# Memory heads: sample rows turned by VectorE and DMA, the sample memory update moved behind the outputs, and the last key block's high and low queries in one matmul

## The chip, the core and the metric

The kernel runs on one core of a Trainium2 chip. TensorE (PE) multiplies, VectorE (DVE), ScalarE (ACT) and GpSimd (POOL) compute elementwise, and SyncE (SP) issues nearly all DMAs from one in-order queue. The metric is the device time of one execution in microseconds (us); lower is better. All data are 32-bit floats. A product that needs more precision than one pass of the matmul gives is made of three: each factor is split into a high part (the rounded value, names ending in `h`) and a low part (the rest, names ending in `l`), and high x high, high x low and low x high are accumulated.

## The reference

One step of a one-layer streaming encoder over 512 prompt rows and 32 sample rows (they come ahead of the prompt rows, so each tile has 544 columns, T). The change lies in the mLSTM branch, four heads of 512 channels each:

```python
s = jnp.einsum('bhtd,bhsd->bhts', q, k) * dmat
num = w_inter[..., None] * jnp.einsum('bhed,bhtd->bhte', C, q) + jnp.einsum('bhts,bhse->bhte', s, v)
den = w_inter * jnp.einsum('bhd,bhtd->bht', n, q) + jnp.sum(s, axis=-1)
h = num / jnp.maximum(jnp.abs(den), jnp.exp(-m_t))[..., None]
C_new = decay[..., None, None] * C + jnp.einsum('bhs,bhse,bhsd->bhed', w_last, v, k)
```

Here `dmat` holds the decays and is zero for keys later than the query, `C` and `n` are the memory, and `w_inter`, `w_last` and `decay` weigh old memory against new. The prompt starts from an empty memory; the sample has a given one (`C0`). Each head's output `h` is then normalised over its 512 channels, scaled, gated by `z` and multiplied by `w_brm`. The new memories of the prompt (`Cp`) and of the sample (`Cs`) are outputs too.

## The kernel before

Channels lie on the 128 partitions and rows along the free axis; a head has KH = 4 channel tiles `f` and NB = 4 blocks `b` of 128 prompt rows. The heads run one after the other. A head makes its decays (`stage_decay`), keys and queries (`stage_k`, `stage_q`), scores (`stage_scores`), and then its memory chain `mchain(h, pump)`, followed by `stage_br`, the product with `w_brm`.

PE's order is written out by hand. `mchain` is a generator: each `yield n` lets the pump emit n steps of the input projection, about six matmuls of 272 columns each (tile `d`, line 575, 455 for the first head's last), before the chain's next piece. So the tables of gaps (KTGAP, KWGAP, VTGAP, GAPS) set how much projection work stands between two pieces of the chain. The order on the other engines is made by a scheduler from the program's order and priorities. The projection's weights arrive as raw pieces (`wi..r`, line 172, on SP), are summed and split on DVE (lines 508 and 205) and ACT (line 204) and then multiply.

The pieces of a head, in PE's order, with the tiles that the traces name:

- `sc` (line 1054): the scores, one group for each of the four key blocks. Block j has as many query columns as remain behind it: 512, 384, 256 and, for the last, 128. Each group is 12 matmuls: 4 channel tiles times the 3 pairs of high and low. DVE multiplies by the decays (`dm`, line 1062).
- `vt` (line 1210): the prompt's values, turned from channels-on-partitions to rows-on-partitions by PE, four 128x128 transposes for each of 4 blocks; ACT evicts the high part `vh` (line 1213), DVE the low part `vl` (line 1214). They go through two double banks (`paux`), so that a block's transposes wait for the evictions of the block two ahead.
- `vts` (line 1222): the same for the 32 sample rows. POOL first writes them three times side by side (`thrice`, line 963, into `vsm`), so that four transposes give 96 rows, from which `vs` (line 1226 and following) is made, a factor of `Cs` and of the sample's output.
- `nm` (lines 1313, 1289, 1287): the outputs of the prompt's four row blocks and of the sample. `Cs` (line 1241): the sample's memory update, 8 single matmuls a head into a bank of the ring `pd` (shared with `d`); DVE adds each to the old memory (line 1243) and SP stores it (line 1245). In the function `new_memory` they are put between the `nm` matmuls.
- DVE and ACT make the normalisation from the sums (lines 1264 to 1347).
- `C` (line 1112): the prompt's memory. Heads 1 and 2 run it between output and normalised output, with keys fetched by `fetch` (line 1155) and weighed by `parted` (line 1146); head 0 before the outputs, and head 3 in another place.
- `yt` (lines 1366, 1367): the normalised outputs turned back to channels-on-partitions, for each channel tile four transposes of the prompt's blocks and one of the sample's; DVE scales and adds them to `c` (lines 1372, 1373) and multiplies by the gate (line 1374).

## Time and profile before

| | |
|---|---|
| median of 3 runs | 1096.51 us (1095.8 to 1096.66) |
| profiled execution | 1097.29 us, span 1095.6 us |
| granted TensorE clock | 0.999 of full speed |
| PE busy | 1086.1 us, 8765 instructions |
| DVE busy | 920.7 us |
| ACT busy | 684.8 us |
| POOL busy | 180.9 us |
| four heads with their chains | about 90 to 590 us of the span |

A row of a timeline gives the start in us, the duration, the engine, the line and operation, the written and read tiles with their shape, how many instructions were merged, and in brackets the idle time just before, with what ended it. Matmuls are pipelined: a 272-column matmul lasts 0.28 us in the trace while the next begins 0.12 us after it. So what a matmul costs PE is read from the distance of two starts, not from its duration, and the bracket shows a stall's length less that overlap.

### The profile page before, as it was taken

Reading aid. Unit: us, or ns where it says so; the run is one execution under the profiler, and the core shown is the slowest. Engines: PE = TensorE matmul, PEld = TensorE weight load, DVE = VectorE, ACT = ScalarE, POOL = GpSimd, SP = SyncE. Lnnn points to the kernel's source line nnn. Section 1 sums busy time; section 2 is a strip of 40 time slices with the busy share of each in tenths; the row PEclk is TensorE's granted clock in tenths of the full one; section 3 lists DMA queues with packets and bytes.
Section 4 is the critical chain, followed back from the end, with each engine's and each line's share of the span. In section 5 each row is a group of like instructions: output and inputs, shape, how many; then the busy total and the mean of one; then the engine's idle time right before and its main releaser. Section 6 shows DMA issues by size and latency. Waiting matters only on the chain.

```text
span 1095.6 us, 23704 instructions
## 1 busy us (share of the span) xinstructions
PE 1086.1 (99%) x8765; PEld 1075.6 (98%) x8765; DVE 920.7 (84%) x1991; ACT 684.8 (63%) x1545; POOL 180.9 (17%) x417
## 2 busy tenths in 40 slices
PE   9999999999999999999999999999999999999998
PEld 9999999999999999999999999999999999999998
DVE  6986999669798697886899699999999888789885
ACT  6686656645666465665565367777777767445762
POOL 2212014211020120201300123322332100000000
PEclk9999999999999999999999999999999999999999
DMA  6233225533366344374356322222222343443743
GB/s 225 78 97 100 91 87 166 140 106 118 122 182 181 85 145 145 101 244 112 129 186 210 110 78 77 64 84 77 85 77 74 121 158 117 122 129 116 256 146 121
DMA packets 104780, 138.67 MB, mean 127 GB/s; under 512 B 35764, under 2 KB 43572, under 8 KB 104664
## 3 DMA queue, kind: packets, MB, share of 16 engines
q1 hardware_dynamic: 104496, 137.10, 40.2%
q8 instruction: 69, 1.13, 0.4%
q14 instruction: 47, 0.39, 0.1%
q10 hardware_dynamic: 168, 0.06, 0.0%
HBM read 110.96 MB, written 26.16 MB: 125 GB/s over the span
## 4 chain that ended last, share of the span: by engine, by line
PE 76%; DVE 3%; issue 1%; DMA 0%; ACT 0%; POOL 0%; ACTq 0%; DVEq 0%; POOLq 0%
PE d L575 39%; PE ya L229 6%; PE pg L2100 4%; PE yb L229 4%; PE C L1112 3%; PE q L229 3%; PE pl L1816 2%; PE k L229 2%; PE sc L1054 2%; PE nm L1313 2%; PE ple L229 1%; DVE ws L508 1%; PE su L1913 1%; PE ho L1936 1%; PE ht L1896 1%
## 5 line engine op out<-in xcount | busy, mean ns | idle before, releaser
L592 ACT COPY t<-d 128x272 f32<-128x272 f32 x126 | 47.5, 377 | 22.2 <-PE d L575 22.1
L1771 ACT COPY kmos<-hkq 128x256 f32<-128x256 f32 x56 | 24.0, 429 | 50.6 <-DVE hkq L1837 42.9
L1837 DVE TENSOR_TENSOR hkq<-hkq,hq 128x288 f32<-128x288 f32 (+1 forms) x96 | 41.5, 438 | 1.7
L801 DVE SCALAR_TENSOR_TENSOR cv<-ub,vec,cv 128x547 f32<-128x547 f32 x48 | 37.1, 782 | 0.4
L1816 PE MATMUL pl<-hkq,kmos 128*128 128x128 f32 x224 | 34.8, 276 | 0.0
L1816 PEld LDWEIGHTS pl<-hkq,kmos 128*128 128x128 f32 x224 | 30.1, 189 | 0.4 <-ACT kmos L1771 0.4
L1112 PE MATMUL C<-vh,kwl 128*128 128x256 f32 x96 | 27.0, 281 | 0.0
L1112 PE MATMUL C<-vl,kwh 128*128 128x256 f32 x96 | 26.9, 280 | 0.0
L1112 PE MATMUL C<-vh,kwh 128*128 128x256 f32 x96 | 26.8, 279 | 0.0
L963 POOL COPY vsm<-vt 128x96 f32<-128x96 f32 x16 | 16.4, 1035 | 58.6 <-DVE vt L599 43.9
L1853 DVE COPY_PREDICATED at<-lmask,pl 128x256 f32<-128x256 uint8 x56 | 24.9, 444 | 0.0
L1392 DVE TENSOR_TENSOR y<-ya,y 128x272 f32<-128x272 f32 x48 | 18.8, 435 | 7.0 <-PE ya L229 6.7
L1313 PE MATMUL nm<-vh,sh 128*128 128x256 f32 x80 | 22.6, 283 | 0.4 <-ACT Co L1124 0.4
L793 POOL COPY uo<-ub 128x3 f32<-128x3 f32 x16 | 17.8, 1112 | 30.6 <-DVE ub L601 23.5
L1313 PE MATMUL nm<-vl,sh 128*128 128x256 f32 x80 | 22.5, 282 | 0.0
L1313 PE MATMUL nm<-vh,sl 128*128 128x256 f32 x80 | 22.5, 281 | 0.0
L1324 ACT COPY y<-nm 128x516 f32<-128x516 f32 x16 | 9.4, 589 | 20.9 <-PE nm L1313 20.9
L1068 ACT CAST sh<-dm 128x512 fp32r<-128x512 f32 (+3 forms) x16 | 7.3, 459 | 22.8 <-DVE dm L1062 22.8
L1054 PE MATMUL sc<-q,kh 128*128 128x512 f32 (+3 forms) x80 | 18.6, 321 | 0.0
L1243 DVE SCALAR_TENSOR_TENSOR c<-c,wi,Cs 128x256 f32<-128x256 f32 (+1 forms) x32 | 15.0, 474 | 4.1 <-PE Cs L1241 4.0
L1112 PEld LDWEIGHTS C<-vh,kwh 128*128 128x128 f32 x96 | 18.1, 189 | 0.0
L1112 PEld LDWEIGHTS C<-vl,kwh 128*128 128x128 f32 x96 | 18.1, 188 | 0.0
(5764 smaller groups left out, 5141.4 us busy)
## 6 DMA issues: line engine op xcount, KB each, us to landing
ya_d<-y SPq DMA_DIRECT2D x32, 272.0 KB, 3.0
y<-ya_d SPq DMA_DIRECT2D x24, 272.0 KB, 3.0
c<-in_C SPq DMA_DIRECT2D x16, 258.0 KB, 3.5
out_Cs<-c SPq DMA_DIRECT2D x16, 258.0 KB, 2.6
out_Cp<-Co SPq DMA_DIRECT2D x15, 258.0 KB, 2.7
k_d<-kf SPq DMA_DIRECT2D x48, 68.0 KB, 2.0
x<-in_xT SPq DMA_DIRECT2D x8, 272.5 KB, 4.6
ya<-ya_d SPq DMA_DIRECT2D x8, 272.0 KB, 4.3
```

The source lines that it names most:

```text
L229: PE.matmul(both[b][:m, :TH], part(w, off + k * step, m, x), xx[:, half(b)], start=(k == 0 and j == 0), stop=(k == n - 1 and j == 2),)
L575: PE.matmul(ps, ww[:, c], xx, start=(start and k == 0 and j == 0), stop=end, skip_group_check=not start,)
L592: S.copy(t, ps)
L801: last = V.scalar_tensor_tensor(cv[:, :547], ub[:, j : j + 547], vcol(V_CW + 4 * ft + j), cv[:, :547], ALU.mult, ALU.add)
L1054: PE.matmul(pn[:, 0, :n], ks[f][x][:, j * P : (j + 1) * P], qs[f][y][:, NS + j * P : T], start=(f == 0 and i == 0), stop=(f == KH - 1 and ...
L1112: PE.matmul(pn[g], kw[b][x][:, f * P : (f + 1) * P], vv[b][y][:, VS[g]], start=(b == 0 and j == 0), stop=(b == NB - 1 and j == 2),)
L1313: PE.matmul(pn[:, g, VP[g] : VP[g] + VN[g]], st[j][x][:, (i - j) * P : (i - j + 1) * P], vv[j][y][:, VS[g]], start=(j == 0 and q == 0), st ...
L1771: S.copy(km.rearrange("p (n j c) -> p n j c", j=2, c=c), view(kk, HB, ((2 * c, NA // (2 * c)), (c - HB, 2), (1, c))),)
L1816: PE.matmul(pn[:, b * P : (b + 1) * P].rearrange("p (n j c) -> p j n c", j=2, c=c), km[:, b * P : (b + 1) * P], view(qq, b * P, ((HB + c, ...
L1837: V.tensor_tensor(x, x, t, ALU.mult)
L1853: V.copy_predicated(blocks2(at[:, :NA]), twice(lmask[:, li, :P]), blocks2(pn[:, :NA]))
L2100: PE.matmul(ps, part(w, k * P, P, x), xx[:, c], start=(k == 0 and j == 0), stop=(k == KD - 1 and j == 2))
```

## The change

1. **Sample values.** In heads 1 to 3 the `vts` transposes and POOL's three copies go. DVE turns the sample columns of each value tile in 32x32 blocks (`V.transpose`, 128x32, 4 a head); four DMAs write them to DRAM (`vs_d`) so that they lie row by row, and three DMAs read these 32 rows into three stripes of 32 partitions (`vr`). `vs` is made from `vr`. Head 0 keeps its transposes.
2. **Sample outputs.** In all heads the fifth transpose of each `yt` group goes. DVE turns the normalised sample block in place (32x512, one a head); one DMA writes it to DRAM (`ys_d`) and one reads it back as four channel tiles (`ys`). Line 1373's scaling now reads `ys`.
3. **Order in heads 1 and 2.** The eight `Cs` matmuls leave the `nm` loop. A table ORDER spreads them, the fetch and weighing of the keys, the four `C` blocks and the read of `ys` among the projection steps behind `nm`.
4. **Last key block.** Where a high and a low query tile lie side by side in one tile (all four channel tiles in head 0, two in the others), one matmul of 256 columns takes both against the high key; the low key's remains with 128. The two halves of the bank are then added: ACT copies one (`dl`), DVE adds the other.
5. **Gaps.** One step fewer or more at several places (KTGAP, VTGAP of heads 0 and 1, GAPS, the `yield` ahead of the old memory's split).

```diff
-FIRSTK, KTGAP, KWGAP = (3, 2, 1, 1, 1), (6, 14), (6, 3, 11)
-VTGAP = ((2, 1, 1, 1, 1), (1, 1, 1, 1, 1), (1, 1, 1, 1, 1), (0, 2, 2, 1, 1))
-GAPS = (20, 20, 20, 14)
+FIRSTK, KTGAP = (3, 2, 1, 1, 1), (4, 14)
+VTGAP = ((2, 1, 2, 1, 1), (1, 1, 2, 1, 2), (1, 1, 1, 1, 1), (0, 2, 2, 1, 1))
+GAPS, CGAP = (18, 20, 20, 15), 1
+YREAD = 8
+VSREAD = 2
+ORDER = (
+    ("fetch", 1),
+    ("cs", 1),
+    ("cs", 1),
+    ("cs", 1),
+    ("cs", 3),
+    ("cs", 2),
+    ("cs", 1),
+    ("cs", 2),
+    ("part", 0),
+    ("cs", 3),
+    ("mem", 0),
+    ("mem", 0),
+    ("reads", 5),
+    ("mem", 0),
+    ("mem", 0),
+)
+LASTGAP = 3
...
+        dl = d2[:, 384 + NS : 512 + NS]
...
-                qh, ql = pair_tile(f"q{i}", 1)
+                both = xp.tile([P, 2 * T], F32R, tag="x1", name=f"q{i}")
+                qhl = both.rearrange("p (a t) -> p a t", a=2)
+                qh, ql = both[:, :T], both[:, T:]
...
+            beside = [f for f in range(KH) if j == NB - 1 and qs[f][2] is not None]
+            for f in beside:
+                PE.matmul(
+                    pn[:, 0, : 2 * P].rearrange("p (a t) -> p a t", a=2),
+                    ks[f][0][:, j * P : (j + 1) * P],
+                    qs[f][2][:, :, NS + j * P : T],
+                    start=(f == 0),
+                    stop=(f == beside[-1]),
+                )
             for f in range(KH):
                 for i, (x, y) in enumerate(((0, 0), (0, 1), (1, 0))):
+                    if f in beside and x == 0:
+                        continue
                     PE.matmul(
                         pn[:, 0, :n],
                         ks[f][x][:, j * P : (j + 1) * P],
                         qs[f][y][:, NS + j * P : T],
                         start=(f == 0 and i == 0),
                         stop=(f == KH - 1 and i == 2),
+                        skip_group_check=bool(beside),
                     )
             with tc.high_priority():
-                V.tensor_tensor(dj[j], pn[:, 0, :n], dj[j], ALU.mult)
+                if beside:
+                    S.copy(dl, pn[:, 0, n : 2 * n])
+                    V.tensor_tensor(dl, pn[:, 0, :n], dl, ALU.add)
+                V.tensor_tensor(dj[j], dl if beside else pn[:, 0, :n], dj[j], ALU.mult)
...
+    ys_d = [dr.tile([HD, NS], F32, name=f"ys_d{h}") for h in range(MH)]
+    vs_d = [dr.tile([NS, HD], F32, name=f"vs_d{h}") for h in range(MH)]
...
+        if h:
+            vq = small("vsm", [P, KH, 3, NS], bufs=1)[:, :, 0]
+            for f in range(KH):
+                V.transpose(vq[:, f], vt[f][:, :NS])
+            to = vs_d[h].rearrange("t (f q e) -> t f q e", f=KH, e=NS)
+            for q in range(P // NS):
+                nc.sync.dma_start(to[:, :, q, :], vq[q * NS : (q + 1) * NS])
         for b in range(NB):
             yield VTGAP[h][b]
+            if h and b == VSREAD:
+                vr = slot(f"vr{h}")[: 3 * NS, :HD]
+                for i in range(3):
+                    nc.sync.dma_start(vr[i * NS : (i + 1) * NS], vs_d[h])
...
-        pt = paux(f"vts{h}")
-        vsm, copied = triple(vt, "vsm", t["copied"])
-        for f in range(KH):
-            PE.transpose(pt[: 3 * NS, 0, f * P : (f + 1) * P], vsm[:, f], ident)
+        if h == 0:
+            vr = paux(f"vts{h}")[: 3 * NS, 0, :]
+            vsm, copied = triple(vt, "vsm", t["copied"])
+            for f in range(KH):
+                PE.transpose(vr[:, f * P : (f + 1) * P], vsm[:, f], ident)
         vs = small("vs", [3 * NS, VW], F32R, bufs=1)
         with tc.high_priority():
-            S.copy(vs[:, :HD], pt[: 3 * NS, 0, :])
+            S.copy(vs[:, :HD], vr)
...
-        yield 4
+        yield 5
...
-            G.memset(ysm[:, :HD], 0.0)
...
-                if parts and i and (h or i > 1):
+                if parts and i > (1 if h == 0 else 0) and not turns:
...
+            V.transpose(ysm[:NS, :HD], ysm[:NS, :HD])
+        nc.sync.dma_start(ys_d[h].rearrange("(n e) t -> e n t", e=NS), ysm[:NS, :HD].rearrange("p (n t) -> p n t", t=NS))
...
+        def fetch_all():
             for b in range(NB):
                 fetch(b)
-            yield KWGAP[0]
+        def weigh_all():
             for b in range(NB):
                 parted(b)
-            yield KWGAP[1]
-            for f in range(KH):
-                for _ in memory(h, f, kw, vv):
-                    pass
+        def one_memory():
+            for _ in memory(h, blocks.pop(0), kw, vv):
+                pass
+        def turned_sample():
+            ys = slot(f"ys{h}")[:, : KH * NS]
+            nc.sync.dma_start(ys.rearrange("p (f t) -> p f t", f=KH), ys_d[h].rearrange("(f p) t -> p f t", p=P))
+            return [ys[:, f * NS : (f + 1) * NS] for f in range(KH)]
+        todo = {
+            "fetch": fetch_all,
+            "part": weigh_all,
+            "mem": one_memory,
+            "cs": lambda: new_memory(*parts.pop(0)),
+            "reads": lambda: ysmp.extend(turned_sample()),
+        }
+        ysmp = []
+        if 0 < h < MH - 1:
+            for name, gap in ORDER:
+                if gap:
+                    yield gap
+                todo[name]()
+        else:
+            yield GAPS[h] - YREAD
+            ysmp = turned_sample()
 
         hs = []
         for f in range(KH):
-            yield max((KWGAP[2] if 0 < h < MH - 1 else GAPS[h]) if f == 0 else 1, pump.when["z", f] - pump.done)
+            yield max((LASTGAP if 0 < h < MH - 1 else YREAD) if f == 0 else CGAP, pump.when["z", f] - pump.done)
             ft = h * KH + f
             pt = paux(f"yt{ft}")
             for b in range(NB):
                 PE.transpose(pt[:, 0, b * P : (b + 1) * P], yb[b][:, f * P : (f + 1) * P], ident)
-            PE.transpose(pt[:, 1, :P], yb[NB][:, f * P : (f + 1) * P], ident)
...
-            V.scalar_tensor_tensor(c[:, :NS], pt[:, 1, :NS], g, c[:, :NS], ALU.mult, ALU.add)
+            V.scalar_tensor_tensor(c[:, :NS], ysmp[f], g, c[:, :NS], ALU.mult, ALU.add)
```

How the instructions stand after the change (the digits behind a tile's name are head and tile; those behind the underscore are buffers).

PE, head 1, within the outputs; before:

```order
L1313 MATMUL nm11_3983<-vh10_3809,sl10_3411 128x260
L1241 MATMUL Cs100_3990<-vs_3905,kws_3532 128x256
L1313 MATMUL nm11_3983<-vh11_3827,sh11_3428 128x256
L1313 MATMUL nm11_3983<-vl11_3828,sh11_3428 128x256
L1313 MATMUL nm11_3983<-vh11_3827,sl11_3429 128x256
L1313 MATMUL nm11_3983<-vh11_3827,sh11_3428 128x260
L1313 MATMUL nm11_3983<-vl11_3828,sh11_3428 128x260
L1313 MATMUL nm11_3983<-vh11_3827,sl11_3429 128x260
L1241 MATMUL Cs101_3999<-vs_3905,kws_3532 128x260
L1313 MATMUL nm12_4009<-vh10_3809,sh10_3410 128x256
```

PE, head 1, behind the outputs, where the `Cs` matmuls stand now:

```order
L595 MATMUL d361_3705<-xh3_613,ws436l_3922 128x272
L1295 MATMUL Cs100_4185<-vs_3931,kws_3521 128x256
L595 MATMUL d381_3893<-xh0_525,wa1238h_3944 128x272
L595 MATMUL d381_3893<-xl0_526,wa1238h_3944 128x272
L595 MATMUL d381_3893<-xh0_525,wa1238l_3945 128x272
L595 MATMUL d381_3893<-xh1_529,wa1238h_3944 128x272
L595 MATMUL d381_3893<-xl1_530,wa1238h_3944 128x272
L595 MATMUL d381_3893<-xh1_529,wa1238l_3945 128x272
L1295 MATMUL Cs101_4198<-vs_3931,kws_3521 128x260
L595 MATMUL d381_3893<-xh2_533,wa1238h_3944 128x272
```

Each pair of `Cs` had six `nm` matmuls between it; now the distances are 6, 6, 18, 12, 6, 12 and 18 projection matmuls, and the first stands 12 projection matmuls behind the last `nm`. Head 2 has the same distances.

PE, head 1, the scores of the last key block; before (two rows stand for two matmuls each):

```order
L1054 MATMUL sc13_3448<-q10_3206,kh100_3027 128x128 x2
L1054 MATMUL sc13_3448<-q10_3206,kl100_3028 128x128
L1054 MATMUL sc13_3448<-q11_3238,kh101_3066 128x128 x2
L1054 MATMUL sc13_3448<-q11_3238,kl101_3067 128x128
L1054 MATMUL sc13_3448<-qh12_3282,kh110_3117 128x128
```

and now:

```order
L1078 MATMUL sc13_3453<-q10_3211,kh100_3032 128x256
L1078 MATMUL sc13_3453<-q11_3243,kh101_3071 128x256
L1089 MATMUL sc13_3453<-q10_3211,kl100_3033 128x128
L1089 MATMUL sc13_3453<-q11_3243,kl101_3072 128x128
L1089 MATMUL sc13_3453<-qh12_3287,kh110_3122 128x128
```

Twelve matmuls became ten in heads 1 to 3 and eight in head 0.

SP, head 1, around the way of the sample's outputs; before:

```order
L1128 DMA out_Cp<-Co10_4272 128x516
L172 DMA wi10r1_4452<-in_w_in 128x512
L172 DMA wbm10r0_4758<-in_w_brm 128x512
L1128 DMA out_Cp<-Co11_4300 128x516
L1128 DMA out_Cp<-Co12_4328 128x516
L1128 DMA out_Cp<-Co13_4356 128x516
L172 DMA wbm10r512_4760<-in_w_brm 128x512
```

and now:

```order
L1167 DMA out_Cp<-Co10_4386 128x516
L1167 DMA out_Cp<-Co11_4414 128x516
L1402 DMA ys_d1_140<-y14_4082 32x16x32
L192 DMA wbm11r0_4853<-in_w_brm 128x512
L192 DMA wbm11r512_4855<-in_w_brm 128x512
L1421 DMA ys1_4461<-ys_d1_140 128x4x32
L192 DMA wbm12r0_4941<-in_w_brm 128x512
L1167 DMA out_Cp<-Co12_4488 128x516
L1167 DMA out_Cp<-Co13_4516 128x516
```

The write and the read of the sample's outputs stand behind two stores of the prompt's memory and ahead of the other two, with raw pieces of `w_brm` between them. PE has 38 matmuls fewer in all, DVE 20 instructions more, ACT 4 more, POOL 16 fewer, and SP 29 DMAs more.

12 lines of the change are left out of this document (7 added, 5 removed).

## The prediction

> **What bounds the kernel now.** I read the page first: the busy line and the chain that ended last.
>
> ```profile
> span 1095.6 us, 23704 instructions
> PE 1086.1 (99%) x8765; PEld 1075.6 (98%) x8765; DVE 920.7 (84%) x1991; ACT 684.8 (63%) x1545; POOL 180.9 (17%) x417
> PE 76%; DVE 3%; issue 1%; DMA 0%; ACT 0%; POOL 0%; ACTq 0%; DVEq 0%; POOLq 0%
> ```
>
> PE is busy in 99% of the span and carries most of the chain. So a PE instruction that goes is worth the distance to the next start, and every other edit is worth the PE stall it ends or makes. DVE, with 84%, is the engine that can turn into the bound in one stretch or another. Then I read PE's waits.
>
> ```profile
> PE vt L1210 <- DVE vl L1214: 1.4, 3, 0.7
> PE Cs L1241 <- DVE c L1243: 0.9, 2, 0.7
> ```
>
> Of PE's waits these two, `vt` and `Cs`, stand where the change moves something. The view counts only time in which PE shows nothing at work. A matmul lasts 0.28 us while the next starts 0.12 us behind it, so each stall is longer by starts, and short ones do not appear at all. I therefore size them from the timelines.
>
> **The change part by part.** Everything is summed from starts.
>
> *Scores of the last key block.* PE's timeline in head 3, the end of the third group, the start and the end of the fourth:
>
> ```profile
> 520.35 0.28 PE L1054 MATMUL sc<-qh,kh 128*128 128x256 f32 x1
> ...
> 521.05 0.33 PE L1054 MATMUL sc<-q,kh 128*128 128x128 f32 x2
> ...
> 522.34 0.47 PE L1073 MATMUL scs<-qf,ksm 128*96 128x32 f32 x4
> ```
>
> Six of 256 columns take 521.05 - 520.35 = 0.70 us, 0.117 each. Twelve of 128 columns take 522.34 - 521.05 = 1.29 us, 0.1075 each. The change takes away 20 of the narrow and adds 10 of the wide: 20 x 0.1075 - 10 x 0.117 = 0.98 us less. Half the columns hardly save time here, and that is why joining two pays.
>
> A rule speaks against this. The Trainium skill, "TensorE: Matmul & The Clock Gate", section "Part 2: What happens when you issue a matmul", says that a stream of matmuls costs its columns, one a cycle, 55.6 ns measured for 128. By it a wide matmul costs two narrow ones and this term would be 0, the time 1 us longer than mine. The rows above disagree with it (107.5 against 117 ns), and I take the rows.
>
> *Transposes.* Head 3, the sample's values and two groups of the outputs:
>
> ```profile
> 551.47 0.28 PE L575 MATMUL d<-xh,wa1146l 128*128 128x272 f32 x1
> 551.61 0.61 PE L1222 MATMUL vts<-ident,vsm 128*96 128x128 f32 x4
> 551.97 0.38 PE L575 MATMUL d<-xfh,ws144h 128*128 128x272 f32 x1
> 552.19 0.29 PE L575 MATMUL d<-xfl,ws144h 128*128 128x272 f32 x1
> ...
> 579.76 0.60 PE L1366 MATMUL yt<-ident,y 128*128 128x128 f32 x4
> 580.20 0.27 PE L1367 MATMUL yt<-ident,y 128*128 128x128 f32 x1
> 580.23 0.37 PE L575 MATMUL d<-xh,wa1248h 128*128 128x272 f32 x1
> ```
>
> From 551.47 to 552.19 are 0.72 us, of which two `d` at 0.12 (a row of windows below: 235 instructions in 28.00 us) would take 0.24; a `vts` group costs 0.48, three of them 1.44. Five `yt` take 0.47 and four `vts` 0.36: the fifth is worth 0.11, sixteen of them 1.76. So the PE work that goes is 0.98 + 1.44 + 1.76 = 4.18 us.
>
> *New memory of heads 1 and 2.* First and last `Cs` in the `nm` loop of head 1, then of head 2, each with the first stall and the `d` that follows the loop:
>
> ```profile
> 262.31 0.28 PE L1313 MATMUL nm<-vh,sh 128*128 128x260 f32 x1
> ...
> 262.67 0.28 PE L1241 MATMUL Cs<-vs,kws 96*128 96x256 f32 x1
> ...
> 263.92 0.39 PE L1241 MATMUL Cs<-vs,kws 96*128 96x260 f32 x1 [0.25 <-DVE c L1243]
> ...
> 273.12 0.28 PE L575 MATMUL d<-xfh,wa2236h 128*128 128x272 f32 x1
> ...
> 409.69 0.28 PE L1241 MATMUL Cs<-vs,kws 96*128 96x256 f32 x1
> ...
> 411.34 0.39 PE L1241 MATMUL Cs<-vs,kws 96*128 96x260 f32 x1 [0.65 <-DVE c L1243]
> ...
> 420.38 0.28 PE L575 MATMUL d<-xfh,wa2240h 128*128 128x272 f32 x1
> ```
>
> Between 262.67 and 273.12 lie 74 matmuls, 8 `Cs` and 66 `nm`. At 0.12 (three from 262.31 to 262.67) they need 8.88 us and take 10.45: 1.57 lost. In head 2 the same 74 take 10.69: 1.81 lost. Together 3.38 us. The reason is that each `Cs` waits until DVE has read the one before it, and six `nm` give it only 0.72 us while DVE is also at work on the sums of `y`. The change puts 6 to 18 projection matmuls between them. What it costs there, by a `Cs` with its eviction in the timeline and two stretches of the view by windows (length, then busy us and count of PE, its weight loads, DVE, ACT and POOL):
>
> ```profile
> 270.24 0.28 PE L1241 MATMUL Cs<-vs,kws 96*128 96x260 f32 x1
> 270.56 0.48 DVE L1243 SCALAR_TENSOR_TENSOR c<-c,wi,Cs 128x260 f32<-128x260 f32 x1 [1.12 <-PE Cs L1241]
> 246.00:262.00 16.00, 15.71 (x130) 15.50 (x129) 15.75 (x28) 11.16 (x23) 4.78 (x9) 1.00 0.29 98
> 274.00:302.00 28.00, 28.00 (x235) 28.00 (x234) 20.02 (x58) 19.06 (x35) 2.09 (x9) 1.00 0.38 123
> ```
>
> DVE, waiting for nothing else, starts 0.32 us behind a `Cs` and takes 0.48: a round of about 0.86 with the hand-over. A `Cs` and six `d` give 7 x 0.12 = 0.84 us, three times a head, a tie; 12 and 18 give 1.6 us and more. DVE is busy 20.02 of 28 us behind the outputs, so it will often be free. Its keys' weighing (`kwl`, 0.75 us each, four) stands among the evictions and may hold one. From below 0 (all on time), from above 0.9 a head (one whole round lost); I take 0.25 a head, 0.5 in all, nearer the lower end because of the free DVE. Net 2.9 us gained.
>
> *Values.* Two stalls that the added steps cover, and one that nothing covers:
>
> ```profile
> 256.04 0.28 PE L575 MATMUL d<-xfh,ws336l 128*128 128x272 f32 x1
> 256.61 0.66 PE L1210 MATMUL vt<-ident,vt 128*128 128x128 f32 x4 [0.28 <-DVE vl L1214]
> 257.02 0.37 PE L575 MATMUL d<-xh,wa1138h 128*128 128x272 f32 x1
> 257.23 0.28 PE L575 MATMUL d<-xl,wa1138h 128*128 128x272 f32 x1
> ...
> 115.61 0.66 PE L1210 MATMUL vt<-ident,vt 128*128 128x128 f32 x4 [0.40 <-DVE vl L1214]
> ...
> 402.42 0.66 PE L1210 MATMUL vt<-ident,vt 128*128 128x128 f32 x4 [0.74 <-DVE vl L1214]
> ```
>
> From 256.04 to 257.23 are 1.19 us where an undisturbed group of four takes 0.72: 0.47 lost. Its bracket shows 0.28, so the starts lose about 0.18 more than a bracket; head 0 lost 0.40 + 0.18 = 0.58, head 2 0.92. Heads 0 and 1 get another step, about 0.75 us of projection, ahead of the third block. I book 1.05 us for the two. Head 2's gaps are as before; I book nothing, and keep 0.92 as a possible gain.
>
> *DVE's added work.* Prices of the nearest forms:
>
> ```profile
> L1373 DVE SCALAR_TENSOR_TENSOR c<-yt,vec,c 128x32 f32<-128x32 f32 x16 | 3.8, 246 | 0.0
> L975 DVE STREAM_TRANSPOSE kf<-kf 128x544 f32<-128x544 f32 x12 | 8.9, 738 | 0.5
> ```
>
> A 128x32 transpose is taken as 0.25 us, four a head 1.0; the one of 32x512 as 0.7; the add of 128x128, between the two in size, as 0.3. Around the values DVE is full (15.75 of 16 us), so up to 1.0 us a head, 3 in all, could reach PE through the weights; nothing if DVE has caught up until then, as its 20.02 of 28 us behind them lets it. I take 0.4. ACT's four copies and POOL's lighter load lie beside PE's work, for 0.
>
> *The DMA trips.* Written pieces are 128 bytes long. The nearest are the keys' trip with pieces as short (KB each, us to landing), the wait that SP can add (in total, times, longest), and the time between the last scaling of head 1's outputs and the first use of the sample's:
>
> ```profile
> k_d<-kf SPq DMA_DIRECT2D x48, 68.0 KB, 2.0
> kr<-k_d SPq DMA_DIRECT2D x9, 64.0 KB, 4.2
> SPq L172 <- DVE ws L533: 58.3, 20, 5.8
> 285.17 1.44 DVE L1347 TENSOR_SCALAR y<-y,stat,rs 128x512 f32<-128x512 f32 x3
> 301.32 0.24 DVE L1373 SCALAR_TENSOR_TENSOR c<-yt,vec,c 128x32 f32<-128x32 f32 x1
> ```
>
> The sample's output is normalised at about 286.6 and needed at 301.3, 14.7 us later. The trip is 0.7 (turning) + 2.0 + 4.2 = 6.9 us and leaves 7.8 for SP. The values' rows have the same 6.2 us of trip, and from the first `vt` block to the first use of `vs` PE has more than 100 instructions at 0.12, 12 us. I book 0, and from above a late read is the rival below.
>
> *Sum.* -4.18 - 3.38 + 0.5 - 1.05 + 0.4 = -7.7 us. The profiled execution took 1097.29, so it would be 1089.6; it lay 0.8 above the median of 1096.51, which gives 1088.8. With the best ends (-0.5, -0.4, -0.92) 1087.0; with the `Cs` rounds at 1.8, DVE's work at 2.0 and half of the `vt` gain 1092.2.
>
> **The rivals.** *The stalls move.* Only the PE work goes. The `Cs` rounds, now between weight preparation and `kwl` on DVE, lose as much as before, and `vt` waits likewise: 1096.5 - 4.2 = 1092.3. For it: three of the seven distances are a tie. Against it: DVE's free third there.
>
> *DVE bounds the values' stretch.* With 15.75 of 16 us busy, the heads' d stream would go as fast as DVE makes weights. Then what PE saves just ahead of and in this stretch (scores 0.98, `vts` 1.44, `vt` 1.05) is waited away and 1.0 us a head comes on top: -1.76 - 3.38 + 0.5 + 3.0 = -1.6, or 1094.9. For it: the full window. Against it: PE lost only 0.29 us of 16 in that window.
>
> *Slower: the sample's output comes late.* The four scalings that read `ys` stand on DVE ahead of those of the prompt. If the read, queued on SP behind two memory stores and raw pieces, is late, DVE stands, with it the gates and splits that `stage_br` multiplies, and weights. One SP wait of the raw pieces' longest kind (5.8) at the write and one at the read make 11.6, 3.8 more than the 7.8 us free. In four heads this is 15.2 - 7.7 = 7.5 us slower, 1104. It decides from 1.9 us a head, 9.7 us of SP waits. Against it: both waits would have to be long in each head.
>
> The Trainium skill, "DMA: Bandwidth & Descriptors", section "Specifications", says that transfers below 512 bytes are read, modified and written; were the trip longer by that, this rival would gain. The keys' writes of that size landed in 2.0 us, so the trace shows no such loss.
>
> **How the numbers follow.** This kernel's measurement tells 0.2%, 2.2 us, from no change. My forecast, 1087.0 to 1092.2, has 0.62; moved stalls 0.16; DVE's bound 0.12 (0.08 of it within 0.2%, the rest just faster); the late output 0.10, of which 0.02 is small enough to end within 0.2%. Faster 0.82, same 0.10, slower 0.08. The range from 1086.0 to 1095.0 takes in the first three and leaves out the slow one.
>
> **What would show it.** PE's busy time some 4 us lower with 38 instructions fewer; `sc` of 256 columns in the last group 0.117 apart; `nm` in heads 1 and 2 without a bracket and the loop 8 `Cs` and the stalls shorter; `Cs` among `d` with brackets below 0.2; no `vt` wait in heads 0 and 1. Wrong it would be if DVE rows show idle time ended by the DMA into `ys` or `vr`, if PE's `d` rows wait for weights around the values, or if `Cs` still loses more than 1 us a head.

## The result, and the profile after

| | before | after the change |
|---|---|---|
| median, runs on the same chip | 1096.15 us (1095.28 to 1096.66, 6 runs) | 1090.97 us (1089.94 to 1092.76, 6 runs) |
| ratio | | 0.995, 95% interval 0.9938 to 0.9962 |
| profiled execution | 1097.29 us, span 1095.6 | 1091.37 us, span 1089.4 |

The change is worth 5.2 us; 7.7 were forecast. The time of 1090.97 lies 2.2 above the point of the forecast, inside its range. On another chip the same kernel gave 1090.33 against 1095.45 (0.9957, 0.9944 to 0.9971).

The page of the changed kernel, the span and the busy line, then its view of PE's waits (total, times, longest, in us):

```profile
span 1089.4 us, 23703 instructions
PE 1081.3 (99%) x8727; PEld 1071.7 (98%) x8727; DVE 923.9 (85%) x2011; ACT 689.0 (63%) x1549; POOL 166.9 (15%) x401
```

```profile
PE warm L1533 <- DVE emc L1320: 1.1, 1, 1.1
PE d L595 <- DVE h L619: 0.8, 1, 0.8
PE nm L1366 <- ACT Co L1163: 0.8, 1, 0.8
PE d L595 <- DVE t L661: 0.6, 1, 0.6
PE k L249 <- ACT kf L1018: 0.3, 1, 0.3
PE d L595 <- DVE z L619: 0.3, 1, 0.3
```

The 38 matmuls are gone and PE's busy time is 4.8 us lower. `Cs` and `vt` no longer stand among the waits. New are two waits of `d` for DVE, 0.8 and 0.6; they lie in the output projection, far behind the change. The wait of `nm` for ACT's `Co`, in head 0, is 0.8 where it was 0.4.

To see where the time went I cut PE's timeline at the first matmul of each head's product with `w_brm`. In the changed kernel these are

```profile
169.29 0.29 PE L249 MATMUL ya<-hm0h,wbm000h 128*128 128x272 f32 x1
...
314.11 0.29 PE L249 MATMUL ya<-hm4h,wbm100h 128*128 128x272 f32 x1
...
457.73 0.29 PE L249 MATMUL ya<-hm8h,wbm200h 128*128 128x272 f32 x1
...
580.21 0.29 PE L249 MATMUL ya<-hm12h,wbm300h 128*128 128x272 f32 x1
```

and in the kernel before, profiled a second time,

```profile
170.73 0.29 PE L229 MATMUL ya<-hm0h,wbm000h 128*128 128x272 f32 x1
...
586.37 0.29 PE L229 MATMUL ya<-hm12h,wbm300h 128*128 128x272 f32 x1
```

with 317.66 and 463.93 between them. The first profile of before has the four starts at 170.88, 318.60, 465.87 and 588.31. Head 0 is counted from the first `sc`, 93.05 in the first profile of before, 93.23 in the second, 93.04 after. The last two columns are head 3's product itself (first to last `ya`) and the output projection (last `yb` to first `pg`). All in us, by starts. The four heads hold the same number of `d` matmuls in every row. `e3`, `m_cs`, `g_gaps` and `g_eighteen` are experiments told below.

| | head 0 | head 1 | head 2 | head 3 | its product | output projection |
|---|---|---|---|---|---|---|
| before, first profile | 77.83 | 147.72 | 147.27 | 122.44 | 23.57 | 50.88 |
| before, second profile | 77.50 | 146.93 | 146.27 | 122.43 | 23.57 | 51.00 |
| after | 76.25 | 144.83 | 143.62 | 122.47 | 24.08 | 52.66 |
| after, second profile | 76.97 | 144.38 | 143.63 | 122.80 | 24.09 | 51.01 |
| e3 | 76.12 | 144.55 | 143.65 | 122.79 | 24.09 | 50.61 |
| m_cs | 77.75 | 145.63 | 144.80 | 122.44 | 23.57 | 50.94 |
| g_gaps | 77.41 | 150.33 | 144.84 | 122.50 | 23.57 | 50.61 |
| g_eighteen | 77.24 | 145.37 | 144.57 | 122.50 | 23.57 | 50.61 |

Between the two first profiles the four heads are 8.1 us shorter (588.31 to 580.21), a little more than the 7.7 forecast. Three things stand against reading that as success: the second profile of before has the heads 2.1 us shorter already; head 3 gained nothing, its product even lost 0.5; and the output projection lost 1.8.

### The profile page after: what moved, and what is told of

Its sections match the earlier page's. It is cut to its first block, busy times and chain, and to the rows that moved or that the text cites. A ratio compares the mean times of both kernels' runs of the same rounds, so it can differ in the third digit from the quotient of the medians.

```text
span 1089.4 us, 23703 instructions
## 1 busy us (share of the span) xinstructions
PE 1081.3 (99%) x8727; PEld 1071.7 (98%) x8727; DVE 923.9 (85%) x2011; ACT 689.0 (63%) x1549; POOL 166.9 (15%) x401
## 4 chain that ended last, share of the span: by engine, by line
PE 93%; DVE 4%; ACT 2%; issue 1%; DMA 0%; ACTq 0%; DVEq 0%
PE d L595 42%; PE ya L249 8%; PE pg L2180 4%; PE yb L249 4%; PE q L249 4%; PE k L249 4%; PE C L1151 3%; PE nm L1366 3%; PE pl L1896 2%; PE u L375 2%; PE v L249 2%; PE sc L1089 2%; PE d L475 2%; PE ple L249 1%; PE su L1993 1%
## 5 line engine op out<-in xcount | busy, mean ns | idle before, releaser
L1896 PEld LDWEIGHTS pl<-hkq,kmos 128*128 128x128 f32 x224 | 30.1, 189 | 0.4 <-ACT kmos L1851 0.4
L814 POOL COPY uo<-ub 128x3 f32<-128x3 f32 x16 | 10.1, 628 | 67.1 <-DVE ub L619 28.3
L341 POOL COPY ub<-vec 128x3 f32<-128x3 f32 x16 | 4.7, 292 | 94.4 <-PE vt L1263 31.0
L1151 PEld LDWEIGHTS C<-vh,kwl 128*128 128x128 f32 x96 | 18.1, 188 | 0.0
L1848 POOL COPY early<-hkq 128x64 f32<-128x64 f32 x32 | 10.5, 327 | 48.2 <-DVE hkq L1917 29.1
L813 POOL COPY uo<-ub 128x3 f32<-128x3 f32 x16 | 13.9, 868 | 24.4 <-DVE ub L621 9.4
```

Of the source, the lines that this page charges most:

```text
L1151: PE.matmul(pn[g], kw[b][x][:, f * P : (f + 1) * P], vv[b][y][:, VS[g]], start=(b == 0 and j == 0), stop=(b == NB - 1 and j == 2),)
L1896: PE.matmul(pn[:, b * P : (b + 1) * P].rearrange("p (n j c) -> p j n c", j=2, c=c), km[:, b * P : (b + 1) * P], view(qq, b * P, ((HB + c, ...
```

## The experiments

The theories to tell apart were, first, why the output projection lost time; then which part of the change earned what.

### The lost time in the output projection: e1_again, e2_dram, e3_weigh, e4_phase

In the changed kernel's timeline (start, duration, engine, line; in brackets the idle time before and what ended it) ACT, which at this point weighs the last head's keys (line 2223) between splits of weights, waits for a load:

```profile
1002.79 1.44 SPq L2218 DMA_DIRECT2D xl<-k_d  x3
1005.18 1.37 ACT L2223 ACTIVATE xh<-xl,col 128x512 fp32r<-128x512 f32 x2 [1.99 <-PE d L595]
1009.16 0.72 ACT L2223 ACTIVATE xh<-xl,col 128x512 fp32r<-128x512 f32 x1 [2.62 <-DMA xl<-k_d]
1011.62 0.36 PE L595 MATMUL d<-yfh,ws33h 128*128 128x272 f32 x1 [0.58 <-DVE t L661]
...
1014.15 0.37 PE L595 MATMUL d<-yfh,ws13h 128*128 128x272 f32 x1 [0.81 <-DVE h L619]
```

Three loads of 256 KB leave together. Two have landed when ACT wants them, the third lands about 5.8 us after its issue and holds ACT for 2.62 us; the weight split behind it is late, and PE stands twice. The change touches nothing here, so either the new DRAM tiles lie in the way, or the instruction stream's phase, or it is chance.

e1_again is the changed kernel once more, on the chip of the other three.

> The changed kernel once more, unaltered. In its first profile the heads came out 8.1 us shorter (first product with w_brm of head 3 at 580.21 us against 588.31), but 0.5 us went at that product and 1.8 us in the output projection at about 1011 to 1016 us, where PE waited for weights that ACT split late behind the weighing of the keys, whose load from k_d took 5.8 us instead of 4.0. If that loss belongs to the program (where its code loads or its DRAM tiles fall), this profile shows it again within 0.3 us and the time stays at 1091. If it is chance of one execution, the load lands in about 4 us here, PE loses under 0.4 us there, and the time spreads between 1089 and 1091.

Measured: 1090.33 us (1089.91 to 1092.35) against 1095.45, ratio 0.9957 (0.9944 to 0.9971). In its profile the same load holds ACT for less than a third of that time, and no `d` has a bracket:

```profile
1005.82 1.57 ACT L2223 ACTIVATE xh<-xl,col 128x512 fp32r<-128x512 f32 x2 [1.91 <-PE d L595]
1008.21 0.73 ACT L2223 ACTIVATE xh<-xl,col 128x512 fp32r<-128x512 f32 x1 [0.81 <-DMA xl<-k_d]
```

The output projection takes 51.01 us, as before. The 1.8 us are a property of that one execution, not of the kernel.

e2_dram declares the new DRAM tiles behind the old ones, so that the old keep their addresses:

```diff
-    ys_d = [dr.tile([HD, NS], F32, name=f"ys_d{h}") for h in range(MH)]
-    vs_d = [dr.tile([NS, HD], F32, name=f"vs_d{h}") for h in range(MH)]
     v_d = dr.tile([NB, 2, P, VW], F32, name="v_d")
     k_d = [dr.tile([T, HD], F32, name=f"k_d{h}") for h in range(MH)]
+    ys_d = ...
+    vs_d = ...
```

> The changed kernel with the new DRAM tiles ys_d and vs_d allocated behind v_d and k_d instead of ahead of them, so that k_d lies where it lay before the change; nothing else moves. If the place of k_d in DRAM makes its load late, the ACT wait at the key weighing falls from 2.6 us to about 0.8 and the time to 1089.2. If code loads or chance do it, the ACT wait stays above 2 us and the time at 1091.

Measured: 1090.2 us, 0.9953 (0.9941 to 0.9966); the output projection took 51.24. No difference from e1_again. But the late load had stayed away in the unaltered program too, so this run can't tell whether the place in DRAM has to do with it.

e3_weigh takes the weighing of these keys out of the projection's way. It is issued behind the activation of a later unit, so that ACT does not stand at it:

```diff
...
-        if n % NB == 3:
+        if n % NB == 1:
             wc = col[:, 10 + b, MH - 1 : MH]
-            S.mul(kh, raw, wc)
-            V.scalar_tensor_tensor(kl, raw, wc, kh.bitcast(F32), ALU.mult, ALU.subtract)
+            with tc.issue_after(act.ins):
+                S.mul(kh, raw, wc)
+                V.scalar_tensor_tensor(kl, raw, wc, kh.bitcast(F32), ALU.mult, ALU.subtract)
```

> The changed kernel with head 3's key weighing (ACT's and DVE's two instructions a block) queued behind the gates of the last product, where nothing waits for it, instead of ahead of the splits of output weights. Whatever makes the load late, PE cannot wait for it any more: the stalls at 1011 and 1014 us (0.74 and 0.98 by starts) go, 1.8 us, and the time falls to about 1089.2. If the stalls come from something else, they stay and the time is 1091.

Measured: 1089.03 us (1088.41 to 1090.2), 0.9942 (0.993 to 0.9954). The output projection takes 50.61 us, 0.4 less than in e1_again, and PE has no wait there. g_gaps and g_eighteen reach the same 50.61 without this edit, so the 0.4 is not shown to be its work. It is 1.3 us below e1_again on the same chip, but the intervals overlap. It is the base of the experiments that undo parts of the change.

e4_phase shifts the phase of the instruction stream: 46 matmuls of 4 columns behind the warm-up ones at the start.

```diff
+        for _ in range(46):
+            PE.matmul(wps[:, 0, :4], warm, warm[:, :4], start=True, stop=True)
```

> The changed kernel with 46 more matmuls of 4 columns at PE's start (they compute nothing that is used). PE's code comes in pieces of 16 KB, one for about 256 instructions; 92 more put its loads back to where they fell before the change. The time itself rises by the 46 matmuls, 2 to 5 us, so what counts is the load of the keys and PE's stalls 430 us behind the first product with w_brm of head 3. If the code loads delay the key load, ACT's wait there falls to about 0.8 us and PE's loss to 0.3. If DRAM place or chance do it, it stays above 2 us, or is unrelated.

Measured: 1108.78 us (1107.1 to 1111.63), 1.0123 (1.0107 to 1.0139). The late load did not come back (0.92 us of ACT's wait); as it was absent from e1_again too, this says nothing of the phase. What made this run longer than e1_again, 18.5 us by the medians and 21.7 by the two profiled executions, are the added matmuls and a slower start behind them (last section):

```profile
1.10 3.78 PE L1533 MATMUL warm<-warm 128*128 128x128 f32 x16 [1.10 <-DVE emc L1320]
4.68 19.63 PE L1535 MATMUL warm<-warm 128*128 128x4 f32 x92
24.17 0.80 PE L375 MATMUL u<-x00h,wf0h 128*128 128x272 f32 x2
```

The trace has two passes for each. The 92 take 24.17 - 4.68 = 19.5 us, 0.212 each, nearly as much as the 16 of 128 columns ahead of them (4.68 - 1.10 = 3.58, 0.224 each).

### The kernel before, profiled again: b1_before

> The kernel before once more, for a second profile. The first one took 1097.29 us while its timed runs have a median of 1095.45, and it showed PE stalls of 1.34 us at the queries of head 1 (213 us) that the changed kernel has in none of its profiles. If the missing 2.3 us of my forecast (7.7 forecast, 5.1 to 5.2 measured) are chance stalls of that one execution, the span here is 1093.5 to 1094.5, the stall at the queries is under 0.4 us, and the difference of the heads to the changed kernel is 6.5 to 7. If they are not, the span is 1095.6 and the stall is there again.

Measured: 1095.78 us, span 1094.1 against 1095.6 of the first profile. Heads 0 to 2 are 0.33, 0.79 and 1.00 shorter. The start of head 3's product lies 6.2 us behind that of the changed kernel (586.37 and 580.21), somewhat less than the 6.5 to 7 expected. The first profile had, in head 1,

```profile
213.46 0.74 PE L229 MATMUL q<-cs4h,wq110h 128*128 128x272 f32 x2 [0.83 <-DVE q L1031]
```

The second has no bracket there; in head 2 the `vt` stall of 0.74, quoted in the prediction, is absent too. So the profile on which the forecast was made held some 2 us of stalls that another execution of the same kernel does not have. All comparisons below are with the second profile.

### Undoing one part of the change: u_cs, u_yt, u_vts

u_cs puts the `Cs` matmuls of heads 1 and 2 back between the `nm` matmuls; the gaps keep the change's values.

```diff
-                if parts and i > (1 if h == 0 else 0) and not turns:
+                if parts and i > (1 if h == 0 else 0):
                     new_memory(*parts.pop(0))
...
-            "cs": lambda: new_memory(*parts.pop(0)),
+            "cs": lambda: None,
```

> The kernel with the late key weighing (1089.03 us, 0.9942 of before), with the Cs matmuls of heads 1 and 2 back between the outputs; everything else stays. By my theory the waits for DVE come back, 1.57 and 1.81 us less what Cs still loses among the projection: heads 1 and 2 longer by 2.9 us together, the time 1092, 0.997 of before. If the stalls had only moved to other places (first rival), under 1 us.

Measured: 1089.31 us, 0.9947 (0.9934 to 0.9959), no different from e3's 0.9942. The move is worth nothing in this kernel. PE's timeline of head 1 in u_cs:

```profile
263.37 0.28 PE L1295 MATMUL Cs<-vs,kws 96*128 96x256 f32 x1
...
264.19 0.28 PE L1295 MATMUL Cs<-vs,kws 96*128 96x260 f32 x1
...
265.03 0.28 PE L1295 MATMUL Cs<-vs,kws 96*128 96x256 f32 x1
```

They stand in the same places as in before, six `nm` between them, and follow each other at 0.82 and 0.84 us without a stall. In before it was 1.0 to 1.24. What ended the stalls was something else in the change, which led to the runs with gaps alone, below.

u_yt turns the sample's outputs on PE again (the fifth transpose of each `yt` group, no trip through DRAM).

```diff
+            G.memset(ysm[:, :HD], 0.0)
...
-            V.transpose(ysm[:NS, :HD], ysm[:NS, :HD])
-        nc.sync.dma_start(ys_d[h]..., ysm...)
...
+            PE.transpose(pt[:, 1, :P], yb[NB][:, f * P : (f + 1) * P], ident)
...
-            V.scalar_tensor_tensor(c[:, :NS], ysmp[f], g, c[:, :NS], ALU.mult, ALU.add)
+            V.scalar_tensor_tensor(c[:, :NS], pt[:, 1, :NS], g, c[:, :NS], ALU.mult, ALU.add)
```

> The kernel with the late key weighing (1089.03 us, 0.9942 of before), with the sample's outputs turned by PE again and without the trip through DRAM. By my theory sixteen transposes come back, 1.76 us, the time 1090.8, 0.9958 of before. DVE's 5 us of waiting for ys in two heads go; if they cost PE anything (third rival, small), the loss is under 1 us or there is a gain.

Measured: 1091.49 us, 0.9962 (0.9948 to 0.9975) against e3's 0.9942: about 2 us more, the intervals overlapping. In the profile the `yt` groups take 0.44, 0.44, 0.44 and 0.38 us more in the four heads, 1.70 together (from before to after they lost 1.76, as forecast). But head 3 with its product took 145.96 us, against 146.88 in e3: there PE got 0.38 us more work and was still 0.92 faster. In this run and in best the first four `ya` of head 3 stand ahead of its last `yt` group; that is why the head and its product are counted together.

u_vts turns the sample's values of heads 1 to 3 on PE again (`if True:` for `if h == 0:`, without the four writes and three reads).

> The kernel with the late key weighing (1089.03 us, 0.9942 of before), with the sample's values of heads 1 to 3 turned by PE again and POOL's copies, without the seven DMAs a head. By my theory three groups of transposes come back, 1.44 us, the time 1090.4, 0.9955 of before. If DVE bounds the values' stretch (second rival), its relief of 0.2 us a transpose pays it back in part: in head 3, which gained nothing from the change, under 0.2 us; in all 0.5 to 1.0.

Measured: 1090.11 us, 0.9948 (0.9936 to 0.996), no different from e3. The `vts` group costs PE 0.35 us in each head; heads 1 and 2 are 0.50 and 0.46 longer, head 3 is 0.63 shorter.

Part of such a difference belongs to one execution. Head 3 has the same code in after, e1_again, e2_dram, e3_weigh, e4_phase and u_cs; with its product it takes 146.16 us in e4_phase and 146.55 to 147.01 in the other five. In the two profiles of before, m_cs, g_gaps and g_eighteen it takes 146.00 to 146.07. So head 3 lost time, though 0.95 us of PE's work had left it. In e3 its timeline shows two of the places, one ahead of the outputs and one in its product:

```profile
542.71 0.43 DVE L619 TENSOR_TENSOR z<-d,t 128x272 f32<-128x272 f32 x1
...
543.19 0.19 PEld L595 LDWEIGHTS d<-xfh,ws144h 128*128 128x128 f32 x1 [0.32 <-DVE z L619]
```

```profile
581.67 0.68 DVE L225 TENSOR_TENSOR wbm301l<-wbm30r,wbm301h 128x512 fp32r<-128x512 f32 x1
...
582.31 0.73 DVE L167 TENSOR_TENSOR hm15l<-c,hm15h 128x544 fp32r<-128x544 f32 x1
582.41 0.30 PEld L249 LDWEIGHTS ya<-hm14h,wbm301l 128*128 128x128 f32 x2 [0.23 <-DVE wbm301l L225]
```

The first is absent in u_vts and best, the second in u_yt and best. The weight loads' brackets show what PE's own row hides, that PE waited for DVE: there PE goes as fast as DVE makes `z`, `hm` and the low parts of `w_brm`.

The largest loss lies between the two, in the loop of the outputs, and comes from the trip of the values. ACT makes `vs` from `vr`. In e2_dram it waits for that read, and PE then waits for ACT:

```profile
546.13 0.62 ACT L1279 CAST vs<-vr 96x512 fp32r<-96x512 f32 x1 [1.43 <-DMA vr<-vs_d]
...
549.94 0.38 PE L1366 MATMUL nm<-vh,sh 128*128 128x256 f32 x1 [0.51 <-ACT y L1377]
```

In e4_phase, with the same code in this head, it doesn't:

```profile
567.49 0.62 ACT L1279 CAST vs<-vr 96x512 fp32r<-96x512 f32 x1
```

The loop, from the first `nm` of head 3 to the matmul behind the last, takes 10.24 us where this wait of ACT is 0 (e4_phase) or 0.19 (u_yt), 10.62 where it is 0.70 (after), 10.95 and 10.96 at 0.88 and 1.18 (e3, e1_again), 11.07 and 11.02 at 1.26 and 1.43 (u_cs, e2_dram). Without the trip, in u_vts, in best and in the kernels that turn this head's values on PE, it is 10.24 again. SP issues the three reads behind stores of the values; the last of them left 3.3 us ahead of ACT's use in e4_phase and 1.3 us ahead in e2_dram. Why SP was later there is open.

In the changed kernel, the trip of head 3's sample outputs:

```profile
569.11 0.60 PE L1447 MATMUL yt<-ident,y 128*128 128x128 f32 x4
569.20 0.69 DVE L1401 STREAM_TRANSPOSE y<-y 32x512 f32<-32x512 f32 x1
569.92 0.34 SPq L1402 DMA_DIRECT2D ys_d<-y  x1
571.72 0.38 SPq L1421 DMA_DIRECT2D ys<-ys_d  x1
575.48 0.40 DVE L1453 SCALAR_TENSOR_TENSOR c<-ys,vec,c 128x32 f32<-128x32 f32 x2
```

DVE turns the block only when PE has begun the prompt's transposes. The read lands 2.9 us after its issue at the median, at 574.6, and the sample's scalings stand behind it at 575.48 and later, with the gates and splits of `hm` behind them. From the first `yt` to the end of its product head 3 takes 35.16 to 35.18 us in the seven profiles with this trip, and 34.94 in u_yt, which has 0.38 us more of PE's work there. So the trip costs some 0.6 us in this head. Whether the order on DVE or its added work weighs more in this isn't separated.

### Adding one part to the kernel before: m_cs, g_gaps, g_eighteen

m_cs has only the move of `Cs` in heads 1 and 2: the table ORDER without `reads`, the last gap 3 instead of 11, the rest as before.

```diff
-FIRSTK, KTGAP, KWGAP = (3, 2, 1, 1, 1), (6, 14), (6, 3, 11)
+FIRSTK, KTGAP, KWGAP = (3, 2, 1, 1, 1), (6, 14), (6, 3, 3)
+ORDER = (("fetch", 1), ("cs", 1), ..., ("part", 0), ("cs", 3), ("mem", 0), ...)
...
-                if parts and i and (h or i > 1):
+                if parts and i and (h or i > 1) and not 0 < h < MH - 1:
                     new_memory(*parts.pop(0))
```

> The kernel before with the move of Cs in heads 1 and 2 only (the order of keys, weighing, C and Cs behind the outputs), gaps ahead of the outputs as before. By my prediction's step 2.9 us go, 1092.7, 0.9973. By the new theory it is also an own way to the same end: Cs no longer waits between outputs, so 2.5 to 3 us go here too; the two gains do not add. If neither, no change.

Measured: 1093.45 us (12 runs), 0.9976 (0.9967 to 0.9985). Heads 1 and 2 are 1.30 and 1.47 us shorter than in b1_before, 2.8 together; the forecast had 2.9 for this step. Alone, the move does what it was costed at.

g_gaps has only the added steps: one more ahead of the third block of `vt` in heads 0 and 1, one more behind head 1's last, one more ahead of the old memory's split in all heads.

```diff
-VTGAP = ((2, 1, 1, 1, 1), (1, 1, 1, 1, 1), ...)
+VTGAP = ((2, 1, 2, 1, 1), (1, 1, 2, 1, 2), ...)
...
-        yield 4
+        yield 5
```

> The kernel before with two of the change's numbers only: the steps ahead of the value blocks of heads 0 and 1 (VTGAP) and five steps in place of four ahead of the old memory's split; Cs stays between the outputs. With Cs put back there, the changed kernel did not lose the 2.9 us I had booked for the move. New theory: the added steps let the outputs begin where the projection holds one tile of the ring pd less, so that a Cs waits for the Cs two before it and not for the last one. Then this kernel loses none of the 3.38 us of Cs waits nor the 1.0 of vt: heads 1 and 2 3.5 to 4 us shorter than in the second profile of before, the time 1091.5, 0.9965 of before. If the move was what ended them, only the vt waits go: 1 us, 0.999.

Measured: 1097.35 us (12 runs), 1.0009 (1.0 to 1.0018). No gain in time, neither the 1091.5 nor the 1 us that were expected, but two opposite effects in the profile. The `Cs` of heads 1 and 2 have no stalls any more, and head 2 is 1.43 us shorter. Head 1 is 3.4 longer, since the product of head 0 in it takes 28.69 us instead of 23.57:

```profile
172.74 0.51 PE L229 MATMUL ya<-hm2h,wbm001h 128*128 128x272 f32 x2 [0.36 <-ACT hm2h L146]
174.80 0.52 PE L229 MATMUL ya<-hm2l,wbm001h 128*128 128x272 f32 x2 [1.54 <-DVE hm2l L147]
176.15 0.82 PE L229 MATMUL ya<-hm3l,wbm001h 128*128 128x272 f32 x2 [0.29 <-DVE hm3l L147]
```

Head 0's outputs are turned two steps later than before, while their product starts where it did. The change has GAPS of head 0 at 18 instead of 20, which takes these two steps back. g_eighteen adds that:

```diff
-GAPS = (20, 20, 20, 14)
+GAPS = (18, 20, 20, 14)
```

> The kernel before with the added steps of heads 0 and 1 (one more ahead of the third value block, one more behind head 1's last, one more ahead of the old memory's split) and, unlike the run that had only these, with head 0's gap ahead of its turned outputs at 18 instead of 20, as the whole change has it. Theory (the steps alone end the waits of Cs; what the earlier run gave back came from head 0's outputs being two steps late for the product with w_brm): Cs 0.97 us and nm about 9.3 us in heads 1 and 2 as in that run, head 1's segment near 145.5 us instead of 150.3, the w_brm product of head 0 near 23.7 us instead of 28.8, together 2.5 to 3.3 us below the kernel before, about 1093. Rival (the product of head 0 was late for another reason, weights or keys that the steps push back): 5 us stay lost there, the time within 1.5 us of the kernel before, 1095 to 1097.

Measured: 1092.54 us (1090.47 to 1092.89) against 1097.22 on its chip, 0.9958 (0.9945 to 0.9972). The product of head 0 is undisturbed, head 1 takes 145.37, head 2 144.57. Four numbers in two tables and a `yield`, with all 8765 matmuls of before, give 0.42% where the whole change gives 0.50%, and the intervals overlap widely.

Why the steps end the stalls of `Cs` shows in the two timelines of PE and DVE together. Before, second profile:

```profile
261.73 0.28 PE L1241 MATMUL Cs<-vs,kws 96*128 96x256 f32 x1
262.45 0.46 DVE L1243 SCALAR_TENSOR_TENSOR c<-c,wi,Cs 128x256 f32<-128x256 f32 x1
...
262.97 0.39 PE L1241 MATMUL Cs<-vs,kws 96*128 96x260 f32 x1 [0.25 <-DVE c L1243]
```

and g_eighteen:

```profile
263.65 0.28 PE L1241 MATMUL Cs<-vs,kws 96*128 96x256 f32 x1
...
264.40 0.47 DVE L1243 SCALAR_TENSOR_TENSOR c<-c,wi,Cs 128x256 f32<-128x256 f32 x1
264.48 0.28 PE L1241 MATMUL Cs<-vs,kws 96*128 96x260 f32 x1
...
265.32 0.28 PE L1241 MATMUL Cs<-vs,kws 96*128 96x256 f32 x1
```

In before the second `Cs` starts when DVE has read the first (262.45 + 0.46 = 262.91). In g_eighteen it starts at 264.48, while DVE reads the first until 264.87. The other starts say the same: in before six of the seven later `Cs` of heads 1 and 2 start 0.05 or 0.06 us behind the end of the reading of the one just before, in g_eighteen five of seven start up to 0.62 us ahead of it. In head 3 of before, too, five of seven start ahead of it, and six of the seven distances are 0.83 to 0.85, without any added step. That fits a ring `pd`, which `Cs` shares with the projection, with one bank free at the loop's start in before and two with another step; the number of free banks itself is read from these starts. DVE starts 0.7 us behind the first `Cs` in both timelines; with two banks that delay costs PE nothing.

### The best of both: best

e3 with head 3's sample values and outputs turned on PE as before (the trips only in heads 1 and 2, for the outputs 0 to 2).

> The changed kernel with the late key weighing, and with head 3's sample rows (values and outputs) turned by PE as before the change; heads 0 to 2 as changed. In the undo runs head 3 and its product with w_brm came out 0.6 us shorter without the values' part and 0.9 us shorter without the outputs' part. If DVE bounds head 3, both go: 1.0 to 1.5 us less than the 1089.03 us with the late weighing, 1087.8, 0.993 of before, faster than both kernels. If PE bounds it, the 0.9 us of transposes come back and it is 1089.9.

Measured: 1089.56 us (1088.52 to 1090.7), 0.9937 (0.9925 to 0.995), not to be told from e3's 0.9942, and not the 1087.8 expected if DVE bounds the head. In its profile head 3 with its product takes 147.00 us, no less than in e3. The stalls ahead of the outputs, in their loop and at the product's start are gone, but later in the product PE loses 0.94 us by starts to DVE's `y`, which reads the sums of the matmuls before it. DVE was late because it had stood for a raw piece of later weights:

```profile
594.88 0.69 DVE L553 TENSOR_TENSOR ws<-wi64r,wi64r 128x512 f32<-128x512 f32 x1 [4.57 <-DMA wi64r<-in_w_in]
```

This wait is 0.3 to 3.0 us in the other profiles. Without the 0.94 the head would take 146.06, an estimate, much as before the change and in u_yt (146.00 and 145.96). So this profile doesn't contradict the losses above, and the timed runs don't show a gain from ending them.

## Why the prediction came out as it did

Point by point, by its own steps, in us:

| step | forecast | measured |
|---|---|---|
| scores, four heads | -0.98 | -0.95 (0.36, 0.19, 0.18, 0.22) |
| `vts`, three heads | -1.44 | -1.05 by the group (0.35 each); heads 1 and 2 are 0.50 and 0.46 longer with it back (u_vts) |
| fifth `yt` transpose | -1.76 | -1.76 |
| `Cs` in heads 1 and 2 | -2.9 | -2.8 by the move alone, -3.3 by the steps alone, not both |
| `vt` in heads 0 and 1 | -1.05 | both gone from `vt`; a new wait of `nm` in head 0, of a `d` in head 1 |
| DVE's added work | +0.4 | head 3: 0.36 ahead of its outputs, and part of the 0.6 below |
| DMA trips | 0 | little in heads 0 to 2; head 3: 0.4 to 0.8 by the values' in five of six profiles, 0.6 by the outputs' |
| sum against before | -7.7 | -5.2 timed; the heads and the product -5.45 against the second profile of before |

**Scores: right, to 0.03.** PE in head 3 of the changed kernel:

```profile
512.90 0.40 PE L1078 MATMUL sc<-q,kh 128*128 128x256 f32 x2
...
513.99 0.81 PE L1112 MATMUL scs<-qf,ksm 128*96 128x32 f32 x8
```

The group takes 513.99 - 512.90 = 1.09 us where twelve narrow ones took 1.29. The columns in it are the same in number, so the rule of the Trainium skill ("TensorE: Matmul & The Clock Gate", "Part 2: What happens when you issue a matmul") that the prediction named as speaking against this change would give no difference. The rows show 0.20.

**Transposes: sized right on PE, but not all of it reached the time.** From g_eighteen, which has the stalls of `Cs` ended and all of PE's work, to e3, heads 0 to 2 are 1.12, 0.82 and 0.92 us shorter, 2.9 together; their removed work is 0.80, 1.01 and 1.00. There the work that went is about the time that went, though head 0 alone differs by up to 1.3 us between profiles of the same code, and by the timed ratios (0.9958 and 0.9942) the whole step lies inside the intervals. Head 3 with its product is 0.8 longer.

**DVE's added work: fair in size, wrong in place.** The prices were fair or too high: a 128x32 transpose was booked at 0.25 and took

```profile
535.43 0.20 DVE L1251 STREAM_TRANSPOSE vsm<-vt 128x32 f32<-128x32 f32 x1
```

and the 32x512 took 0.69, as booked. The 0.4 was spread over the heads; what shows is in head 3, where the `d` behind DVE's `z` loses 0.36 by starts whenever DVE turns the values, and never when PE does.

**The DMA trips, booked at 0: the step that failed.** For the values the prediction set 6.2 us of trip against 12 us from the first `vt` block to the first use of `vs`. But the reads stand on SP ahead of the third block, behind stores, so what counts is the time from their issue to that use: 3.3 us in e4_phase and 1.3 in e2_dram, for a read that lands 3.4 us after its issue at the median. In head 3 ACT waited for `vr` in five of the six profiles of its changed code by 0.7 us or more, and PE lost 0.4 to 0.8 in the outputs' loop; with the wait at 0 or 0.19 it lost nothing. The outputs' trip cost some 0.6 more. The prediction had named idle time ended by the DMA into `ys` or `vr` as a sign that it is wrong, and took the slack for the outputs from head 1 alone. So PE's savings in head 3, 0.95 us, were waited away, and 0.5 (after) to 0.8 (e3) lost on top of them, against g_eighteen. The rival "DVE bounds the values' stretch" forecast such a loss for three heads and from DVE; it came in one head and in good part from the DMA. Heads 1 and 2 have the four `C` blocks between the outputs and `yt`; that they lost nothing for this reason is argued, not shown.

**Stalls of `Cs`: the number right, the reason wrong.** The prediction said that six `nm` are too short for DVE's answer, and credited the move. The move alone does gain that much (m_cs), but so do the steps that the prediction took for a remedy of `vt` only (g_eighteen), and with those in place the move is worth nothing (u_cs). Two cures of one wait don't add. What limits, as far as the starts show, is the number of banks that are free when the loop begins. The prediction read the wait as a distance and not as a ring with one free bank. Its own +0.5 for late rounds beside `d` hardly shows: `Cs` no longer stands among PE's waits.

**`vt`: half right.** Head 0 has no wait of `vt` any more. In head 1 the stall of 0.47 is gone from `vt`, and a `d` right behind it now has

```profile
256.05 0.39 PE L595 MATMUL d<-xfh,ws136h 128*128 128x272 f32 x1 [0.26 <-DVE z L619]
```

DVE was late, and with the added step PE met another of its results late: 0.43 lost by starts. In head 0 PE now waits for ACT's `Co` ahead of an `nm`: 0.67 to 1.53 us in all eleven profiles with the added steps, 0.37, 0 and 0.29 in the two of before and in m_cs. The steps alone make head 0 only 0.26 shorter (77.50 to 77.24), where 0.58 was booked. That is the rival "the stalls move", in two places of three.

**The late output.** DVE did stand for `ys`, as this rival had it, in heads 1 and 2:

```profile
295.68 0.74 DVE L1453 SCALAR_TENSOR_TENSOR c<-ys,vec,c 128x32 f32<-128x32 f32 x4 [2.46 <-DMA ys<-ys_d]
```

It cost PE little or nothing there: with the transposes back on PE (u_yt) head 2 is 0.86 us longer and head 1 0.13, for 0.44 more work in each. The prediction counted 7.8 us of slack from head 1; in head 3 the read is issued behind the first two `yt` and lands 5.5 us behind the first, and there the trip counts.

**The level.** The sum was set against one profiled execution. That execution held 2.1 us in heads 0 to 2 that the next one hadn't; where they show as stalls (the `q` of head 1, the `vt` of head 2) no booked term contains them; the prediction corrected its level by 0.8, from the profiled time to the median. The changed kernel's own first profile held a similar chance loss, 1.7, in the output projection. So -8.1 in the heads and +1.8 behind them were both partly chance, and only the timed ratio and the second profiles show the change's own size.

Put together: of 7.7, head 3's removed work (about 1.1 as it was booked) was waited away, its new stalls took 0.5 to 0.8, and head 1's `vt` gain (0.47) moved. That leaves 7.7 - 1.1 - 0.65 - 0.47 = 5.5 with the middle of the two, beside 5.2 timed; 0.3 of head 0's `vt` gain went as well. This account is put together after the fact from profiles; single profiles differ by as much as its smaller terms. That the time lies inside the forecast's range is in part luck: the largest term, `Cs`, came out at its size although the move that it was credited to adds nothing beside the added steps.

## What to carry to other kernels

A wait of a matmul for the reading of its predecessor's bank may be a matter of how many banks are free when the loop begins: look at which earlier instruction it waits for, and try one step more ahead of the loop before moving work; two cures for one wait are worth one. Work taken from PE and given to DVE pays in stages where DVE has caught up and is lost where PE's next product is fed by DVE, so price it by stage, head by head. The slack of a trip through DRAM runs from the issue of its read to the use, not from its write: here 1.3 to 3.3 us where 12 were counted. Profile the kernel before twice before sizing stalls below 1 us from it.
